# A transformer layer on one core: a feed-forward that begins with four token tiles, adds its partial products in PSUM and takes the gate a round earlier

## The chip, the core and the metric

The kernel runs on one core of a Trainium2 chip. The metric is device time in microseconds (us) of one execution; of several runs the median is shown. The engines are TensorE (PE, matrix products; PEld is its weight load), VectorE (DVE), ScalarE (ACT), GpSimd (POOL) and SyncE (SP), which issues the DMAs. Each engine works through its own list of instructions in a fixed order and waits on semaphores where it needs another engine's result. PE's results land in PSUM, eight banks of 512 fp32 values for each of 128 partitions; the other buffers are in SBUF, and parts of the program's data go to DRAM and back.

## What is computed

One layer of a diffusion backbone, batch 1, in fp32, for 512 sample tokens and 128 prompt tokens, with D_MODEL 1024 and D_FF 2816. Cut to its skeleton:

```python
mod = silu(cond) @ w_ada + b_ada                        # cond is c for the sample, c_ctx for the prompt
sh1, sc1, gt1, sh2, sc2, gt2 = split(mod, 6)
h = rmsnorm(x, norm_attn) * (1 + sc1) + sh1
q_lat, kv_lat, k_rope, gq, gk, gv, gf_low, gb_low, g_out = split(h @ w_in)
attn = attention(q_lat, kv_lat, k_rope)                 # 8 heads, low-rank keys and values
o = gla(gq, gk, gv, gates) * silu(g_out)                # gated linear attention, both directions
x = x + gt1 * (concat(attn, o) @ w_out)
h2 = rmsnorm(x, norm_ffn) * (1 + sc2) + sh2
a, g = split(h2 @ w_ffn_in, 2)                          # 2 x 2816 columns
x = x + gt2 * ((silu(a) * g) @ w_ffn_out)
y = rmsnorm(x, final_norm)
```

The outputs are y for prompt and sample, and the prompt's latent keys, rotary keys and final states. The change touches the loads of w_ada, the second norm, the feed-forward and the last gate.

## The kernel before

**Tokens and precision.** The 640 tokens are five tiles of 128: 0 to 3 are the sample, 4 is the prompt. Every fp32 factor is split in a rounded high part (a cast on ACT, L219) and a low part (a subtraction on DVE, L220), and a product is three passes: high by high, high by low, low by high (`mm3`, L212 to L214). A matrix product below always counts these passes.

**What sets the order.** The program is first written in a natural order. Then a planner (`Plan`) lays all instructions on the engines with a cost for each (`cost`) and a lag for each semaphore, redraws the order at random TRIES times in windows of 100 us and keeps the shortest; `keep` fixes that order on every engine. So a change in one place or in a cost can move instructions on all engines. SBUF is handed out by allocators: `late` names the ring of split weights that the feed-forward takes turns in (eight slots of 1024, TURNS), `rounded` the split activations, `plain` the rest.

**Up to 380 us.** Loads, adaLN modulation, first norm, input projection, gated linear attention, attention. Then the output projection: its first 512 columns for all tiles, its second 512 columns tile by tile in the order 4, 0, 1, 2, 3, 24 products each. After a tile's second half `residual` runs on DVE (L1365, L1366), then `second_norm(t)`: square with sum on ACT (L1417), the reciprocal root (two scalar steps on ACT, L278, five on DVE, L246 to L250), the scale on ACT (L1419), eight transposes on PE (L1429), scale and shift from PSUM on DVE and ACT (L1437, L1435), and the splits of four right operands (`right_split`; a right operand `right[r]` is a 512 x 320 piece of the normed activations: half of the features, half of the columns of each tile, 64 columns a tile). Differences of the pieces (L1447 to L1450) later give `right` 4 to 7.

**The feed-forward** takes the 2816 hidden columns in 22 pairs j of 128 columns (an a half for the silu and a g half), in rounds of 6, 6, 5 and 5 pairs (PARTS). Of the first CLASSIC pairs (2) each is computed by `whole`: four uses of a weight tile, a0, a1, g0, g1, for each 24 products of 128x320 (two PSUM halves times four k times three passes, L1560), 96 for a pair. All other pairs go through `part`: seven sub-products of 12 each (L1600), r = 1, 2, 6, 7, 5, 4, 3, by the scheme that multiplies 2x2 blocks with seven products, 84 for a pair. Each sub-product has a PSUM bank of its own; DVE adds it to sums in SBUF (L1604, seven per pair), ACT copies the first (L1607), ACT applies silu (L278), DVE multiplies a by g (L1627), and the product is split into hidden columns (`hidden_split`). `weights` splits the weight tiles up to eight uses ahead.

After each round its hidden columns are multiplied with w_ffn_out, 512 output columns at a time (n = 0, 1), with one PSUM bank per tile as accumulator (`mm3`, 128x512). The sums y over rounds are kept in DRAM: the second and third round load, add and store them. In the last round all y are loaded and multiplied by the gate gt2 and added to x (L1645, L1646, five tiles by two halves); n = 0 runs over pairs with all five tiles inside, n = 1 runs tile by tile, each followed by `final`: square (L1740), reciprocal root, one DVE step that scales by it and by final_norm (L1742), and the store. The last tile's n = 1 comes in two parts of 256 columns, with separate squares (L1753). The gate gt2 is made by `ada_gate(5)` in the second round and its vectors are loaded in the last.

## Time and profile before

| | |
|---|---|
| time, median of 3 runs | 831.02 us (830.35 to 831.64) |
| profiled execution | 831.04 us, its span 829.3 us |
| mean granted clock of PE | 0.983 |
| PE busy | 792.4 us, 96% of the span |
| PE weight loads | 703.1 us, 85% |
| DVE busy | 625.1 us, 75% |
| ACT busy | 387.1 us, 47% |
| moved by DMA | 118.17 MB, 142 GB/s in the mean |

The span is the time from the first to the last instruction in the profile; 1.7 us of the execution's time lie around it. A busy PE is not always PE at its peak: its products overlap, so the distance between starts counts, and the clock that the throttle grants it can be half. The chain of waits tells which work set the end at each time; windows tell how busy each engine was in a stretch and which clock PE had. A row of a timeline gives start, length, engine, line, operation, output and input, and in brackets the idle time before it with what ended it.

### The profile page before, as it was taken

The numbers are of one execution on the slowest core, as the hardware profiler recorded it, in microseconds if no ns is written. First come the engines' busy times: TensorE is split into PE (matmuls) and PEld (weight loads), VectorE is DVE, ScalarE is ACT, GpSimd is POOL, SyncE is SP. The second block draws the span as 40 slices with busy tenths as digits, with TensorE's granted clock in tenths as the row PEclk, the third lists the DMA queues.
The fourth block names the chain that finished last, engine by engine and source line by source line (L and its number), as shares of the span: only waits on it lengthen the run. The fifth ranks groups of instructions, "written<-read, shape, count | busy, mean of one in ns | idle before, by whom it ended". The sixth has DMA issues, their size and how long they took to land.

```text
span 829.3 us, 13015 instructions
## 1 busy us (share of the span) xinstructions
PE 792.4 (96%) x4803; PEld 703.1 (85%) x4803; DVE 625.1 (75%) x1252; ACT 387.1 (47%) x770; POOL 5.2 (1%) x15
## 2 busy tenths in 40 slices
PE   8899799899998999997999999999999999999994
PEld 6588787687987877886999988999879998899984
DVE  4689995886657565479888834888988886588897
ACT  6368255144556676258544434445214452245413
POOL 0000000000000000000000000000000000000000
PEclk9999999999999999997999999999999999999998
DMA  9981447327334246544132424333877335432433
GB/s 338 330 258 50 118 130 208 114 70 216 88 82 106 63 127 201 173 159 128 52 102 64 140 89 140 90 115 114 257 214 227 104 112 187 171 103 90 136 106 127
DMA packets 102136, 118.17 MB, mean 142 GB/s; under 512 B 15543, under 2 KB 69937, under 8 KB 102073
## 3 DMA queue, kind: packets, MB, share of 16 engines
q1 hardware_dynamic: 102073, 117.35, 45.6%
q8 instruction: 38, 0.62, 0.3%
q14 instruction: 25, 0.20, 0.1%
HBM read 96.96 MB, written 13.55 MB: 133 GB/s over the span
## 4 chain that ended last, share of the span: by engine, by line
PE 77%; DVE 12%; DMA 6%; ACT 3%; issue 2%; SPq 0%; ACTq 0%; DVEq 0%
PE psum L1600 30%; PE psum L212 10%; PE psum L214 10%; PE psum L213 10%; PE psum L1560 4%; PE psum L889 3%; PE psum L1241 2%; PE psum L1310 2%; DMA plain<-in_w_ada 1%; DVE plain L1646 1%; PE psum L712 1%; DMA plain<-in_w_in 1%; ACT plain L278 1%; DVE plain L1645 1%; PE psum L1296 1%
## 5 line engine op out<-in xcount | busy, mean ns | idle before, releaser
L1600 PE MATMUL psum<-rounded,late 128*128 128x320 f32 x1680 | 247.5, 309 | 0.0
L1600 PEld LDWEIGHTS psum<-rounded,late 128*128 128x128 f32 x1680 | 246.8, 188 | 0.3
L219 ACT CAST late<-plain 128x512 fp32r<-128x512 f32 (+2 forms) x204 | 123.7, 617 | 206.6 <-PE psum L214 78.4
L220 DVE TENSOR_TENSOR late<-plain,late 128x512 fp32r<-128x512 f32 (+3 forms) x204 | 137.8, 683 | 50.9 <-ACT late L219 48.5
L214 PE MATMUL psum<-late,rounded 128*128 128x512 f32 (+1 forms) x225 | 86.6, 385 | 0.0
L213 PE MATMUL psum<-late,rounded 128*128 128x512 f32 (+1 forms) x225 | 86.5, 384 | 0.0
L212 PE MATMUL psum<-late,rounded 128*128 128x512 f32 (+1 forms) x225 | 86.5, 384 | 0.0
L1604 DVE TENSOR_TENSOR plain<-plain,psum 128x320 f32<-128x320 f32 x140 | 66.1, 484 | 23.3 <-PE psum L1600 21.8
L213 PE MATMUL psum<-rounded 128*128 128x512 f32 (+2 forms) x212 | 77.8, 376 | 4.4 <-DVE rounded L220 4.4
L214 PE MATMUL psum<-rounded 128*128 128x512 f32 (+2 forms) x212 | 76.0, 377 | 0.0
L212 PE MATMUL psum<-rounded 128*128 128x512 f32 (+2 forms) x212 | 75.1, 380 | 0.7 <-DVE rounded L552 0.5
L219 ACT CAST rounded<-plain 128x256 fp32r<-128x256 f32 (+5 forms) x91 | 50.7, 582 | 46.1 <-DMA plain<-in_w_in 14.3
L220 DVE TENSOR_TENSOR rounded<-plain,rounded 128x256 fp32r<-128x256 f32 (+5 forms) x91 | 56.7, 642 | 20.5 <-ACT rounded L219 18.5
L278 ACT ACTIVATE plain<-plain 128x1 f32<-128x1 f32 (+7 forms) x111 | 37.9, 349 | 27.4 <-DVE plain L1604 20.7
L214 PEld LDWEIGHTS psum<-late,rounded 128*128 128x128 f32 x225 | 42.3, 188 | 9.2 <-issue 0.8
L212 PEld LDWEIGHTS psum<-late,rounded 128*128 128x128 f32 x225 | 42.3, 188 | 8.3
L213 PEld LDWEIGHTS psum<-late,rounded 128*128 128x128 f32 x225 | 42.3, 188 | 8.3
L213 PEld LDWEIGHTS psum<-rounded 128*128 128x128 f32 x212 | 40.5, 193 | 10.2 <-DVE rounded L220 4.6
L212 PEld LDWEIGHTS psum<-rounded 128*128 128x128 f32 x212 | 40.0, 193 | 8.9 <-DVE rounded L552 1.4
L214 PEld LDWEIGHTS psum<-rounded 128*128 128x128 f32 x212 | 40.6, 194 | 7.7 <-issue 2.5
L1241 PE MATMUL psum<-rounded 96*128 96x320 f32 x192 | 37.3, 322 | 2.5 <-ACT plain L278 1.3
L500 DVE SCALAR_TENSOR_TENSOR plain<-plain 128x1024 f32<-128x1024 f32 x28 | 34.6, 1279 | 0.8 <-DMA plain<-in_w_ada 0.8
(278 smaller groups left out, 1084.9 us busy)
## 6 DMA issues: line engine op xcount, KB each, us to landing
plain<-in_w_ffn_in SPq DMA_DIRECT2D x44, 512.0 KB, 4.7
plain<-in_w_ada SPq DMA_DIRECT2D x26, 512.0 KB, 4.4
plain<-in_w_ffn_out SPq DMA_DIRECT2D x44, 256.0 KB, 3.1
plain<-in_w_ada SPq DMA_DIRECT2D x8, 1024.0 KB, 6.0
y<-plain SPq DMA_DIRECT2D x30, 256.0 KB, 2.9
plain<-y SPq DMA_DIRECT2D x30, 256.0 KB, 3.5
early<-in_w_in SPq DMA_DIRECT2D x7, 512.0 KB, 6.7
early<-in_w_ada SPq DMA_DIRECT2D x6, 512.0 KB, 8.0
```

What stands on the lines that cost most here:

```text
L212: mm(out, lh, rh, start=start, stop=False)
L213: mm(out, lh, rl, start=False, stop=False)
L214: mm(out, ll, rh, start=False, stop=stop)
L219: self.nc.scalar.copy(hi, src).ins,
L220: self.nc.vector.tensor_tensor(lo, src, hi.bitcast(F32), op=ALU.subtract).ins,
L278: i = self.nc.scalar.activation(out, src, func, **more).ins
L500: nc.vector.scalar_tensor_tensor(m.ap, raw.ap, x, m.ap, op0=ALU.mult, op1=ALU.add)
L889: self.nc.tensor.matmul(out, w[:, a], act[:, b], start=start and i == 0, stop=stop and i == 2)
L1241: nc.tensor.matmul(pv[:, n], q[:, a * TS + P * t : a * TS + P * t + P], k[:, b * KEYS + 320 * n : b * KEYS + 320 * n + 320], start=i == 0, ...
L1560: nc.tensor.matmul(pv[:, h], wv[:, k, a], right[:, k, b], start=first and k == 0 and i == 0, stop=not first and k == 3 and i == 2,)
L1600: nc.tensor.matmul(ps, wv[:, k, a], right[:, k, b], start=k == 0 and i == 0, stop=k == 3 and i == 2)
L1604: add = lambda out, x: nc.vector.tensor_tensor(out, x, by_tile(ps), op=ALU.add)
```

## The change

- **Loads of w_ada** by `ada_rest` (two pieces of 1024 columns): 16 of 512 KB in a ring of twice as many half-size buffers, instead of 8 of 1 MB.
- **Column order.** The right operands and hidden columns keep the tiles in the order 4, 0, 1, 2, 3 (ORDER) instead of 0 to 4, so tile 3, which is normed last, has the last 64 of 320 columns.
- **Head.** For the uses a0 and a1 of pair 0 (HEAD), `whole` computes the first 256 columns (four tiles) in 24 products and the last 64 in 24 more.
- **CLASSIC** is 1 instead of 2: pair 1 goes through `part`.
- **Sums in PSUM.** `part` uses three banks per pair: X for r = 1, 6, 5, 3, Z for 7 and 4, Y for 2. A later sub-product adds into the bank of the earlier ones. ACT copies the bank after r = 1, 6 and 7 (`keep`, L1626 of the new kernel); DVE adds a copy after r = 2, 5 and 4 (L1622); after r = 3 the silu reads the bank itself.
- **Gate.** In the third round the sums y are multiplied by gt2 and added to x, which is loaded from and stored to DRAM for it. gt2's vectors are loaded there. The last round has no y.
- **Last round.** All ten weight tiles are split ahead, and each tile runs through both halves of the output columns, then `final`. The last tile has parts of 512, 256 and 256.
- **Planner.** 10 ns more for a product in fp32r, 16 redraws instead of 20.

In the new kernel the line numbers are a little higher: the transposes are L1431, the products of `whole` L1568 and of `part` L1617, the residuals L1367, L1368 and L1669, L1670, the scalings of the second norm L1421, its squares L1419, the shift L1439 and L1437, the multiply of a by g L1649, and `final` has L1764 and L1766.

The places in the order of which the prediction speaks follow. PE between the output projection (L212 to L214) and the feed-forward, before (late_19xx names the weight slot):

```order
L212 MATMUL psum<-rounded 128x512
L1429 MATMUL psum<-plain 128x128
L213 MATMUL psum<-rounded 128x512
L214 MATMUL psum<-rounded 128x512
L1429 MATMUL psum<-plain 128x128 x19
L1560 MATMUL psum<-rounded,late_1913 128x320
L1560 MATMUL psum<-rounded,late_1914 128x320
```

The last 19 transposes, among them those of tiles 2 and 3, stood ahead of every product of the feed-forward. The same place now:

```order
L214 MATMUL psum<-rounded 128x512
L1431 MATMUL psum<-plain 128x128 x8
L1568 MATMUL psum<-rounded,late_1922 128x256 x6
L1431 MATMUL psum<-plain 128x128
L1568 MATMUL psum<-rounded,late_1922 128x256
L1431 MATMUL psum<-plain 128x128 x3
L1568 MATMUL psum<-rounded,late_1922 128x256 x11
L1431 MATMUL psum<-plain 128x128 x2
L1568 MATMUL psum<-rounded,late_1922 128x256 x2
L1431 MATMUL psum<-plain 128x128 x2
L1568 MATMUL psum<-rounded,late_1922 128x256 x4
L1568 MATMUL psum<-rounded,late_1919 128x320
```

Tile 3's eight transposes now stand among the 24 four-tile products of a0; all 256-column products of a1 come behind them. DVE at the same place, from the scalar chain of tile 2's norm (L248 to L250) on, before:

```order
L248 TENSOR_TENSOR plain<-plain 128x1
L249 TENSOR_SCALAR plain<-plain 128x1
L250 TENSOR_TENSOR plain<-plain 128x1
L1437 TENSOR_SCALAR plain<-psum,plain 128x128
L1365 TENSOR_TENSOR plain<-psum,plain 128x512
L1366 TENSOR_TENSOR plain<-plain 128x512
```

and now:

```order
L246 TENSOR_SCALAR plain<-plain 128x1
L247 TENSOR_TENSOR plain<-plain 128x1
L1367 TENSOR_TENSOR plain<-psum,plain 128x512
L248 TENSOR_TENSOR plain<-plain 128x1
L249 TENSOR_SCALAR plain<-plain 128x1
L250 TENSOR_TENSOR plain<-plain 128x1
L1368 TENSOR_TENSOR plain<-plain 128x512
```

Tile 3's residual multiply moved ahead of the last three scalar steps of tile 2. DVE at the end, from the second last tile's scaling on, now (before, two scalings and the residuals of four tiles stood between each other in the last 20 us):

```order
L1766 SCALAR_TENSOR_TENSOR plain<-plain 128x1024
L1669 TENSOR_TENSOR plain<-psum,plain 128x512
L1670 TENSOR_TENSOR plain<-plain 128x512
L1669 TENSOR_TENSOR plain<-psum,plain 128x256
L1670 TENSOR_TENSOR plain<-plain 128x256
L1669 TENSOR_TENSOR plain<-psum,plain 128x256
```

Only the last tile's own residuals stand behind the scaling of the tile before it.

The diff, cut to its core:

```diff
--- before.py
+++ after.py
...
-        src = self.A["w_ada"].rearrange("(h k p) n -> k p h n", h=2, p=P)[:, :, :, D * q : D * q + D]
...
         for k in range(KD // 2):
-            raw = raws.take()
-            rv = raw.rearrange("p (h j c) -> p h j c", h=2, j=2)
-            nc.sync.dma_start(raw.rearrange("p (h n) -> p h n", h=2), src[k])
-            group = []
+            group, two = [], []
             for h in range(2):
+                raw = raws.take()
+                two.append(raw)
+                row = P * (k + KD // 2 * h)
+                nc.sync.dma_start(raw, self.A["w_ada"][row : row + P, D * q : D * q + D])
+                rv = raw.rearrange("p (j c) -> p j c", j=2)
...
-            raws.back(raw)
+            for raw in two:
+                raws.back(raw)
...
-        cols = 64 * t, 64 * t + 64
+        at = 64 * ORDER.index(t)
+        cols = at, at + 64
...
-            out = self.rb.alloc(1024, within=TURNS)
+            out = self.rb.alloc(1024, within=None if r in ROWS and j >= D_FF // P - PARTS[-1] else TURNS)
...
-        for h in range(2):
-            right = self.right[(1, 2, 0, 3)[2 * h + int(r[1])]].v("p (k s t) -> p k s t", k=4, s=2)
-            for k in range(4):
-                for i, (a, b) in enumerate(((0, 0), (0, 1), (1, 0))):
-                    nc.tensor.matmul(
-                        pv[:, h], wv[:, k, a], right[:, k, b],
-                        start=first and k == 0 and i == 0, stop=not first and k == 3 and i == 2,
-                    )
+        starts = []
+        for lo, hi in ((0, HALF - 64), (HALF - 64, HALF)) if (j, r) in HEAD else ((0, HALF),):
+            for h in range(2):
+                right = self.right[(1, 2, 0, 3)[2 * h + int(r[1])]].v("p (k s t) -> p k s t", k=4, s=2)
+                for k in range(4):
+                    for i, (a, b) in enumerate(((0, 0), (0, 1), (1, 0))):
+                        begin = first and k == 0 and i == 0
+                        ins = nc.tensor.matmul(
+                            pv[:, h, lo:hi], wv[:, k, a], right[:, k, b, lo:hi], start=begin and lo == 0,
+                            stop=not first and k == 3 and i == 2, skip_group_check=(0, r) in HEAD,
+                        ).ins
+                        if begin and lo == 0:
+                            starts.append(ins)
+                        elif begin:
+                            self.after(ins, starts[h])
...
-        pb = self.bank()
-        ps = pb.ap[:, :HALF]
+        place = "X" if r in (1, 6, 5, 3) else "Y" if r == 2 else "Z"
+        first, last = r in (1, 2, 7), r in (2, 3, 4)
+        if first:
+            s[place] = self.bank()
+        ps = s[place].ap[:, :HALF]
...
-                    ps, wv[:, k, a], right[:, k, b], start=k == 0 and i == 0, stop=k == 3 and i == 2
+                    ps, wv[:, k, a], right[:, k, b], start=first and k == 0 and i == 0,
+                    stop=k == 3 and i == 2, skip_group_check=not first,
...
+        def keep(x):
+            s[x] = sb.alloc(HALF)
+            nc.scalar.copy(s[x].ap, ps)
         if r == 1:
-            s["u2"] = sb.alloc(HALF)
-            nc.scalar.copy(s["u2"].ap, ps)
+            keep("p1")
             s["a"] = sb.alloc(T)
-        u2 = by_tile(s["u2"].ap)
-        if r == 2:
-            add(side("a", 0), u2)
+        elif r == 2:
+            add(side("a", 0), by_tile(s["p1"].ap))
             self.act(side("a", 0), side("a", 0), AF.Silu)
+            s.pop("p1").free()
         elif r == 6:
-            add(u2, u2)
+            keep("u2")
         elif r == 7:
+            keep("p7")
             s["g"] = sb.alloc(T)
-            add(side("g", 0), u2)
         elif r == 5:
-            add(u2, u2)
-            add(side("g", 1), side("g", 0))
+            add(side("g", 1), by_tile(s["p7"].ap))
+            s.pop("p7").free()
         elif r == 4:
-            add(side("g", 0), side("g", 0))
+            add(side("g", 0), by_tile(s["u2"].ap))
+            s.pop("u2").free()
         elif r == 3:
-            add(side("a", 1), u2)
-            self.act(side("a", 1), side("a", 1), AF.Silu)
+            self.act(side("a", 1), by_tile(ps), AF.Silu)
             f = s["a"].ap
             nc.vector.tensor_tensor(f, f, s["g"].ap, op=ALU.mult)
             self.hidden_split(j, f)
+        if last:
+            s.pop(place).free()
+        if r == 3:
             for x in self.pairs.pop(j).values():
                 x.free()
-        pb.free()
...
+            at = T * s + P * ORDER.index(t)
...
-            if last:
-                for m in self.right.values():
-                    m.free()
+            if p == len(PARTS) - 2:
                 for _ in gate:
                     pass
                 self.cond.free()
                 gt = [sb.alloc(D, True) for _ in range(2)]
                 for c in range(2):
                     nc.sync.dma_start(gt[c].ap, self.rows[1][c : c + 1].partition_broadcast(P))
+            if last:
+                for m in self.right.values():
+                    m.free()
                 fn = sb.alloc(D, True)
...
-                    for n in range(2):
-                        ns = slice(512 * n, 512 * n + 512)
-                        y = sb.alloc(512)
-                        nc.sync.dma_start(y.ap, yd[t][:, ns])
-                        residual(self.x[t].ap[:, ns], t, 512 * n, 512, y.ap)
-                        y.free()
+                self.weights(2 * count - len(self.ready))
+                ws = [self.use() for _ in range(2 * count)]
+                self.act_set(SET_EXP)
+                for t in range(NT):
+                    parts = [512, 512] if t < NT - 1 else [512, *LAST]
+                    done = 0
+                    for n_ in parts:
+                        pb = self.bank()
+                        cs, ys = slice(done % 512, done % 512 + n_), slice(done, done + n_)
+                        for i in range(count):
+                            wv = ws[done // 512 * count + i][1]
+                            self.mm3(
+                                pb.ap[:, :n_], hidden(first + i, 0, t), hidden(first + i, 1, t),
+                                wv[:, 0, cs], wv[:, 1, cs], i == 0, i == count - 1,
+                            )
+                        residual(self.x[t].ap[:, ys], t, done, n_, pb.ap[:, :n_])
+                        pb.free()
+                        done += n_
+                    self.final(t, fn, parts[1:])
+                return
...
                     for t in range(NT):
-                        if last:
-                            residual(self.x[t].ap[:, :512], t, 0, 512, acc[t].ap)
-                        else:
...
+                    y, dst = sb.alloc(512), yd[t][:, 512 * n : 512 * n + 512]
+                    if p == 0:
+                        nc.scalar.copy(y.ap, acc[t].ap)
+                    else:
+                        nc.sync.dma_start(y.ap, dst)
+                        nc.vector.tensor_tensor(y.ap, y.ap, acc[t].ap, op=ALU.add)
+                    if p < len(PARTS) - 2:
+                        nc.sync.dma_start(dst, y.ap)
+                    else:
+                        x, dst = sb.alloc(512), self.xd[t][:, 512 * n : 512 * n + 512]
+                        nc.sync.dma_start(x.ap, dst)
+                        residual(x.ap, t, 512 * n, 512, y.ap)
+                        nc.sync.dma_start(dst, x.ap)
+                        x.free()
+                    y.free()
+                    acc[t].free()
...
+        raws = Ring(sb, 2 * RING, D)
...
-CLASSIC, FIRST_USES, AHEAD_USES, RAW_AHEAD = 2, 3, 8, 8
+ORDER = 4, 0, 1, 2, 3
+HEAD = (0, "a0"), (0, "a1")
+CLASSIC, FIRST_USES, AHEAD_USES, RAW_AHEAD = 1, 3, 8, 8
...
+SWEEPS, TRIES, JITTER, WINDOW = 1, 16, 300, 1e5
...
         c = max(passes * n / 2.4, 53 * passes)
+        if passes == 1:
+            c += 10
...
```

More of the change, by code (lines that the diff above doesn't have):

```diff
@@ L442, in ada_rest @@
                     i = nc.tensor.matmul(
-                        pb.ap[r : r + 32], cv[:, h, k], rv[:, h, j],
+                        pb.ap[r : r + 32], cv[:, h, k], rv[:, j],
                         start=k == 0, stop=k == KD // 2 - 1, tile_position=(0, r),
@@ L1383, in output @@
         self.weights(FIRST_USES)
-        for t in (4, 0, 1, 2, 3):
+        for t in ORDER:
             pb = self.bank(1, ACC)
@@ new lines, in ffn @@
+                return
+            for n in range(2):
+                acc = [self.bank() for _ in range(NT)]
+                for j in range(first, first + count):
+                    self.weights(max(0, AHEAD_USES - len(self.ready)))
+                    w, wv = self.use()
+                    at += 1
+                    for t in range(NT):
+                        self.mm3(
+                            acc[t].ap, hidden(j, 0, t), hidden(j, 1, t), wv[:, 0], wv[:, 1],
+                            j == first, j == first + count - 1,
+                        )
+                    w.free()
+                    if p == GATE_PART:
+                        next(gate, None)
+                for t in range(NT):
+                    y, dst = sb.alloc(512), yd[t][:, 512 * n : 512 * n + 512]
[14 more added lines that the diff above has]
+                    acc[t].free()
@@ L1789, in early @@
         self.z_load(4)
-        raws = Ring(sb, RING, 2 * D)
+        raws = Ring(sb, 2 * RING, D)
         self.gvt = [sb.alloc(512, True) for _ in range(NT)]
@@ L1976 @@
 COLD = 3400
-SWEEPS, TRIES, JITTER, WINDOW = 1, 20, 300, 1e5
+SWEEPS, TRIES, JITTER, WINDOW = 1, 16, 300, 1e5
 def engine(ins):
```

45 lines of the change are left out of this document (1 added, 44 removed).

## The prediction

> **What bounds the kernel now.** I read the chain of waits first, for where the end is set, then PE's groups, then windows and timelines of the places that the change touches. The chain's rows from 389.10 us on (start, us, what):
>
> ```profile
> 389.10 29.63 PE psum L1560 x182
> 420.64 48.84 PE psum L1600 x333
> 722.73 61.61 PE psum L1600 x420
> ```
>
> The feed-forward is PE from its first product to the last rounds. 420 products of 320 columns in 61.61 us are 0.1467 us each. The windows (us, then PE, PEld, DVE, ACT, POOL busy, granted clock, DMA share, GB/s) show no slack in it:
>
> ```profile
> 400.00:500.00 100.00, 100.00 (x610) 94.71 (x609) 74.73 (x137) 43.81 (x83) 0.00 (x0) 1.00 0.30 93
> 500.00:600.00 100.00, 100.00 (x621) 95.49 (x620) 80.09 (x129) 44.63 (x79) 0.00 (x0) 1.00 0.47 144
> 600.00:700.00 100.00, 100.00 (x590) 92.02 (x589) 82.63 (x135) 37.20 (x66) 0.00 (x0) 1.00 0.57 177
> ```
>
> DVE and ACT have room everywhere, so taking adds from DVE is worth nothing by itself here. What is not PE at full speed lies at the two ends. First, the passage from the output projection to the feed-forward, on PE:
>
> ```profile
> 382.01 1.09 PE L1429 MATMUL psum<-plain 128*128 128x128 f32 x8 [1.24 <-ACT plain L1419]
> 385.71 1.97 PE L1429 MATMUL psum<-plain 128*128 128x128 f32 x8 [2.61 <-ACT plain L1419]
> 389.10 11.15 PE L1560 MATMUL psum<-rounded,late 128*128 128x320 f32 x56 [1.42 <-ACT rounded L219]
> ```
>
> PE waits 1.24 + 2.61 + 1.42 = 5.27 us for the norms of tiles 2 and 3, and the last row says that 56 products took 11.15 us where 56 x 0.1467 = 8.2 was due. The granted clock gives the reason, in windows of 3.41 us on the grid on which the clock changes in this trace:
>
> ```profile
> 142.59:146.01 3.42, 2.55 (x26) 0.99 (x18) 1.42 (x2) 3.08 (x4) 0.00 (x0) 1.00 0.76 196
> 146.01:149.42 3.41, 2.29 (x17) 1.74 (x18) 2.76 (x5) 0.77 (x2) 0.00 (x0) 0.98 0.93 309
> 149.42:152.83 3.41, 3.41 (x15) 3.02 (x13) 2.79 (x6) 0.41 (x1) 0.00 (x0) 0.52 0.74 290
> 381.50:384.92 3.42, 1.09 (x8) 0.85 (x8) 3.25 (x13) 3.13 (x8) 0.00 (x0) 0.98 0.69 202
> 384.92:388.33 3.41, 1.97 (x8) 1.57 (x8) 2.96 (x10) 2.88 (x7) 0.00 (x0) 0.50 0.34 109
> 388.33:391.74 3.41, 2.64 (x10) 2.64 (x11) 3.00 (x10) 3.01 (x10) 0.00 (x0) 0.50 0.84 239
> 391.74:395.15 3.41, 3.41 (x15) 3.41 (x14) 3.23 (x11) 0.71 (x2) 0.00 (x0) 0.52 0.29 71
> ```
>
> A window with PE busy 2.29 of 3.41 is followed by half clock, one with 2.55 is not; and of the windows at half clock 2.64 did not bring full clock back, 3.41 did. So PE ran at half speed from 389.10 to about 395.1: 3.0 us lost. The passage costs about 8 us. Second, the tail: PE's last product starts at 818.25 and ends at 818.53, but
>
> ```profile
> 818.25 0.28 PE L214 MATMUL psum<-late,rounded 128*128 128x256 f32 x1
> 796.00:803.00 7.00, 7.00 (x33) 5.79 (x31) 6.86 (x12) 0.00 (x0) 0.00 (x0) 1.00 0.00 0
> 803.00:810.00 7.00, 7.00 (x32) 5.82 (x31) 6.62 (x12) 2.38 (x7) 0.00 (x0) 1.00 0.01 2
> 820.01 1.28 DVE L1742 SCALAR_TENSOR_TENSOR plain<-plain 128x1024 f32<-128x1024 f32 x1
> 822.00 0.41 DVE L1645 TENSOR_TENSOR plain<-psum,plain 128x256 f32<-128x256 f32 x1
> ```
>
> DVE is full there (6.86 of 7) with the residuals of all tiles, and reaches the last piece of the last tile at 822.00, 3.47 us after PE was done. From there to the end of the span, 829.3, are 7.3 us that nothing in the change shortens.
>
> **The change, part by part.** The profiled execution took 831.04 us, the shown median is 831.02, so the sum is made against 831.04. I count PE's time as the moment from which it would have had to run at full speed without a stop.
>
> *Before:* 389.10 + 3.0 = 392.1.
>
> *Earlier start.* The new order puts tile 2's scalar chain on DVE (L248 to L250) behind tile 3's residual multiply (before: ahead of it) and tile 3's square on ACT behind tile 2's scale. These rows price it:
>
> ```profile
> 380.48 0.69 DVE L1365 TENSOR_TENSOR plain<-psum,plain 128x512 f32<-128x512 f32 x1 [0.24 <-PE psum L214]
> 380.81 1.15 ACT L1419 ACTIVATE plain<-plain 128x1024 f32<-128x1024 f32 x1
> ```
>
> Multiply to 381.2, three scalar steps of 0.2 to 381.8, scale 1.15: tile 2's transposes start at about 383.05 instead of 382.01. From a tile's transposes to the first product on it the old row shows 389.10 - 385.71 = 3.39, so the four-tile products of a0 start at about 386.4, 2.7 us sooner than the first product before. PE then has work until tile 3 is normed: 24 products of 256 columns and 8 transposes. Tile 3 itself comes 1 to 1.6 us later than before (about 390.0 to 390.7), and that work lasts longer, since the clock still drops: between 380.9 and 386.4 there are only 1.09 us of work, so whichever way the grid of 3.41 us falls, one window is under half busy. On the old grid the window to 388.33 is again partly idle, the one from 388.33 is full, and full clock is back at 391.74 instead of 395.15. Lost: (391.74 - 386.4) / 2 = 2.7. So 386.4 + 2.7 = 389.1, plus tile 3's eight transposes, now behind the start (1.09), 390.2.
>
> The Trainium skill ("TensorE: Matmul & The Clock Gate", the section on the clock gate and the one on HAM oscillation) has the array fall to half clock after an idle window of about 3.4 us. The trace agrees on the length of the window, not on idle: the longest gap here was 2.61 us and the clock fell. By the page's words it would not fall in the changed kernel; that is rival A.
>
> *Work in the feed-forward.* CLASSIC 1 makes pair 1 seven products of 12 instead of four of 24: 12 products fewer, -12 x 0.1467 = -1.8. The two head products are cut in 256 and 64 columns: 48 products become 96. The price of a product of 64 columns is not in the trace. Bounds, by these rows:
>
> ```profile
> 815.13 0.28 PE L212 MATMUL psum<-late,rounded 128*128 128x256 f32 x1
> 815.25 0.28 PE L213 MATMUL psum<-late,rounded 128*128 128x256 f32 x1
> L461 PE MATMUL psum<-plain x8: 172/253/253, 184.9 to 185.6; 128*128 128x4 f32 x8
> ```
>
> 256 columns start 0.12 apart, and by the step from 320 to 256 columns (0.0267) 64 would take 0.04; eight products of 4 columns, each with its own 128x128 weights, start (185.6 - 184.9) / 7 = 0.10 apart, where the weight load must set it. I take the middle, 0.07: 48 x (0.12 + 0.07 - 0.147) = +2.1, between +0.6 and +3.5. The Trainium skill ("TensorE: Matmul & The Clock Gate", the section on LDWEIGHTS) gives a load of 128 columns 128 / 1.2 = 107 ns; if that set the spacing, the same sum, an estimate by the page, would be +3.8, and the trace's 0.10 for a fresh load of 128 columns is close to it. The start then stands at 390.2 - 1.8 + 2.1 = 390.5: a gain of **1.6** (0.2 to 3.1 by the price of 64 columns).
>
> *Sums in PSUM.*
>
> ```profile
> L1604 DVE TENSOR_TENSOR plain<-plain,psum 128x320 f32<-128x320 f32 x140 | 66.1, 484 | 23.3 <-PE psum L1600 21.8
> ```
>
> Seven such adds per pair become three, and one copy on ACT becomes three. The adds go off an engine that PE did not wait for: 0. But product 6 now adds into the bank of product 1, 5 and 3 into it again, 4 into that of 7. PE must wait until ACT's copy (or DVE's add for 3) has read the bank; one other product lies between, 12 x 0.1467 = 1.76 us. The copy:
>
> ```profile
> 773.80 0.43 ACT L1607 COPY plain<-psum 128x320 f32<-128x320 f32 x1 [0.25 <-PE psum L1600]
> 771.16 1.14 ACT L219 CAST late<-plain 128x512 fp32r<-128x512 f32 x2 [2.17 <-PE psum L1600]
> ```
>
> About 0.25 to hear of PE, 0.43, and as much as 0.25 back: 0.9 when ACT is free, 1.45 with one cast (0.57) before it, 2.0 with two. Behind a late copy stand PE's whole stream, and nothing hides that. ACT is 40% busy and the new order keeps each copy next to its product, so I take +0.3 for the few late ones, from 0 to the price in rival C.
>
> *Gate in the third round.* Ten each of a load, multiply, add and store of 512 columns: 10 x 1.38 = 13.8 us DVE, which had 17.4 us free in 600 to 700 alone; 20 more DMAs of 256 KB where the DMA share is 0.57. Cost 0; if the adds held a bank that the second half's accumulators wait for, one such pair, +1.4. *Last round.* Tile by tile from its start, it needs the last pair's hidden columns after 12 products of 512 columns instead of 60. The rows of that chain:
>
> ```profile
> L278 ACT ACTIVATE plain<-plain 128x320 f32<-128x320 f32 x40 | 18.9, 471 | 20.9 <-DVE plain L1604 20.7
> L1627 DVE TENSOR_TENSOR plain<-plain 128x640 f32<-128x640 f32 x20 | 16.5, 824 | 0.0
> L219 ACT CAST rounded<-plain 128x640 fp32r<-128x640 f32 x22 | 16.0, 727 | 5.7 <-DVE plain L1627 5.7
> 813.65 0.39 PE L213 MATMUL psum<-late,rounded 128*128 128x512 f32 x1
> 814.56 0.39 PE L214 MATMUL psum<-late,rounded 128*128 128x512 f32 x1
> ```
>
> Four steps of 512 columns are 0.91 us, 0.2275 each, so 12 are 2.73. Silu 0.47, multiply 0.82 and cast 0.73 make 2.0, with three hand-overs of 0.25 2.8, and the subtract is needed one product later: +0.2 (0 to 0.8).
>
> *Tail.*
>
> ```profile
> L1646 DVE TENSOR_TENSOR plain<-plain 128x512 f32<-128x512 f32 x19 | 12.9, 691 | 0.6 <-DMA plain<-x 0.2
> 815.46 1.16 ACT plain L1740 x2
> 817.40 0.16 DVE L248 TENSOR_TENSOR plain<-plain 128x1 f32<-128x1 f32 x1
> ```
>
> Each tile now asks DVE for four residual steps of 0.69, the scalar chain (five steps of 0.2, from L246 to L250) and L1742's step (1.28): 5.0 us in the 6.8 of its 30 products, so no backlog. The order still puts the second last tile's L1742 ahead of the last one's residuals. The second last tile's products end 15 x 0.2275 + 30 x 0.12 = 7.0 before PE's end; its residual 1.4, square 1.2, the scalars on ACT and DVE 1.6 and the step 1.28 end 1.5 before it; then 1.4 for the last tile's first half and 0.8 for its third quarter: the last residual starts 0.7 after PE's end, not 3.47. Gain **2.8** (0 if that step comes 3 us later, 3.4 without any backlog).
>
> *Before the output projection*, smaller loads of w_ada and a newly drawn order of every engine. The chain there goes over DVE scans and DMAs:
>
> ```profile
> 84.74 1.49 DVE early L1040
> 94.90 5.39 DMA plain<-in_w_in
> 102.73 4.61 DMA plain<-in_w_in
> ```
>
> The order doesn't shorten a scan or a transfer, so 0; a window more or fewer at half clock is 1.7 us, and two of them are my bound either way, 3.4.
>
> **Sum:** -1.6 + 0.3 + 0.2 - 2.8 = -3.9, so 831.04 - 3.9 = **827.1 us**.
>
> **Rivals.** *A: the clock holds.* The 2.7 us lost at the start are not: 824.4. Against it: 2.29 of 3.41 was too little at 146. 5%. *B: the head gains nothing* (64 columns cost 0.10 and tile 3's norm comes 1 to 2 us later still, so that PE waits again before a1); only the tail pays: 831.04 - 2.8 + 0.5 = 828.7, to 830.5 when DVE's backlog stays in part. For it: DVE and ACT were both about 90% busy (3.25 and 3.13 of 3.42) in that passage, so all added work delays a norm. 16%. *C, the slower side: the banks.* Two casts ahead of a copy make 2.0 against 1.76: 0.25 us, and a copy that is late makes the freed weight tile, hence the next cast, late too. At 0.35 us per pair, 21 pairs, 827.1 + 7.4 = 834.5; it decides against the change from 0.19 us per pair on. For it: casts come in twos on ACT (row 771.16). Against: 60% idle ACT. 12%. *D: the redrawn early order* moves the time by one to two windows: 824 (9%) or 830.5 (9%). The forecast, 825.2 to 828.8, has 49%.
>
> **Numbers.** A measurement of this kernel tells 0.2%, 1.7 us, from no change: faster is below 829.4, slower above 832.7. Faster: 49 + 5 + 9 + 11 of B = 74%. Same: 5 of B + 7 of D = 12%. Slower: C and 2 of D, 14%. The range, 822.8 to 831.5, leaves out C and the ends of D.
>
> **What would show it.** Right: a first product of 256 columns near 386.4; full clock at about 391.7; products of 64 columns 0.05 to 0.09 apart; PE 100% busy from 400 to its end, with no wait of L1617 for L1626 or L1622; the last 256-column residual within 1 us of PE's last product. Wrong: PE idle between the four-tile products and a1 (B); waits of L1617 that come once per pair (C); a feed-forward that starts more than 2 us from 386 because the stages before it moved (D).

## The result: 0.55% slower, and the profile after

| | before | changed |
|---|---|---|
| time, median of 5 runs each | 831.41 us (830.35 to 832.53) | 835.73 us (835.27 to 836.68) |
| ratio to before | | 1.0055, 95% interval 1.004 to 1.0069 |
| span of the profiled execution | 829.3 us | 834.8 us |
| end of the output projection's last product | 380.44 us | 389.53 us |
| from there to PE's last product of all | 438.1 us | 437.6 us |
| from there to the end of the span | 10.8 us | 7.7 us |

The forecast was 827.1 us. The table cuts both traces at two points. Behind the output projection, where all edits of the feed-forward lie, the changed kernel is 3.6 us shorter (448.9 against 445.3). Ahead of it, where the forecast had put a zero with 3.4 us either way, it is 9.1 us longer. Both are read from one execution of each kernel. The last product of the output projection before:

```profile
380.05 0.39 PE L214 MATMUL psum<-rounded 128*128 128x512 f32 x1
```

The timeline of PE in the changed kernel at the passage (start, length, engine, line, operation, count, and in brackets the idle time before):

```profile
389.14 0.39 PE L214 MATMUL psum<-rounded 128*128 128x512 f32 x1
391.95 1.41 PE L1431 MATMUL psum<-plain 128*128 128x128 f32 x8 [2.42 <-ACT plain L1421]
394.88 1.89 PE L1568 MATMUL psum<-rounded,late 128*128 128x256 f32 x6 [1.52 <-ACT rounded L219]
```

Two gaps of 3.9 us together instead of three of 5.27. The windows (us; PE, PEld, DVE, ACT, POOL busy; granted clock; DMA share, GB/s) on the grid of this run's clock, for two places ahead of the output projection, for the passage, and of 100 us each in the feed-forward:

```profile
112.68:116.09 3.41, 1.47 (x3) 0.28 (x4) 3.41 (x11) 3.35 (x17) 0.39 (x1) 1.00 0.50 149
116.09:119.51 3.42, 2.87 (x10) 1.38 (x9) 3.34 (x25) 0.98 (x2) 0.56 (x1) 0.50 0.50 120
119.51:122.92 3.41, 3.41 (x16) 3.32 (x16) 2.73 (x9) 0.22 (x1) 0.00 (x0) 0.50 0.00 0
150.23:153.64 3.41, 0.19 (x4) 0.00 (x0) 0.83 (x1) 1.55 (x2) 0.00 (x0) 1.00 1.03 242
153.64:157.05 3.41, 2.81 (x11) 1.81 (x12) 2.13 (x4) 0.59 (x1) 0.00 (x0) 0.50 1.02 406
157.05:160.47 3.42, 3.42 (x16) 3.14 (x15) 1.40 (x4) 0.00 (x0) 0.00 (x0) 0.50 0.11 43
389.16:392.57 3.41, 0.99 (x8) 0.62 (x7) 3.26 (x12) 3.31 (x8) 0.00 (x0) 1.00 0.13 53
392.57:395.99 3.42, 1.90 (x9) 1.32 (x8) 3.18 (x14) 3.15 (x9) 0.00 (x0) 0.50 0.76 254
395.99:399.40 3.41, 3.41 (x18) 3.41 (x18) 1.89 (x6) 2.15 (x7) 0.00 (x0) 0.50 0.56 156
...
500.00:600.00 100.00, 100.00 (x621) 95.50 (x620) 68.91 (x104) 48.67 (x91) 0.00 (x0) 1.00 0.43 134
600.00:700.00 100.00, 100.00 (x590) 91.94 (x589) 78.09 (x113) 40.73 (x76) 0.00 (x0) 1.00 0.56 173
```

The passage has two windows at half clock instead of three, and the feed-forward is full. But in the early stages two idle stretches (1.47 and 0.19 busy of 3.41) are each followed by two windows at half clock. Over the whole stretch up to the output projection's end six windows are at half clock, before it was three. The groups of waits of PE there, the three longest (total in us, count, longest):

```profile
PE psum L1074 <- DMA plain<-plain: 3.2, 1, 3.2
PE psum L512 <- ACT plain L278: 3.0, 1, 3.0
PE psum L305 <- DMA early<-in_vecs: 2.8, 1, 2.8
```

Before, the longest was another one, and it was longer; so a list of waits alone doesn't show where the 9 us went:

```profile
PE psum L213 <- DVE rounded L220: 4.4, 1, 4.4
```

The steps of the chain behind the first wait of the changed kernel:

```profile
143.05 4.19 DMA plain<-plain
148.90 4.93 DMA plain<-plain
```

These transfers are the moves of the linear attention's gates (L1003, 64x640 values each). Before, the chain had one of them:

```profile
143.03 2.40 DMA plain<-plain
```

The moves go out in pairs, and these rows are not all of the same pair. By the rise of their semaphores the last pair took 2.4 and 2.5 us before and 5.1 and 4.9 now; the pair ahead of it 4.0 and 4.3 before and 3.8 and 4.2 now. So it is the last pair that became slower.

The tail of the changed kernel, the last rows of PE and DVE:

```profile
826.81 0.28 PE L214 MATMUL psum<-rounded 128*128 128x256 f32 x1
824.11 1.28 DVE L1766 SCALAR_TENSOR_TENSOR plain<-plain 128x1024 f32<-128x1024 f32 x1
827.43 0.42 DVE L1669 TENSOR_TENSOR plain<-psum,plain 128x256 f32<-128x256 f32 x1
```

The last residual starts 0.34 us after PE's end at 827.09, not 3.47.

### The profile page after: what moved, and what is told of

Its sections match the earlier page's. It is cut to its first block, busy times and chain, and to the rows that moved or that the text cites. A ratio compares the mean times of both kernels' runs of the same rounds, so it can differ in the third digit from the quotient of the medians.

```text
span 834.8 us, 13004 instructions
## 1 busy us (share of the span) xinstructions
PE 800.6 (96%) x4839; PEld 707.8 (85%) x4839; DVE 603.7 (72%) x1181; ACT 403.3 (48%) x816; POOL 4.8 (1%) x15
## 4 chain that ended last, share of the span: by engine, by line
PE 79%; DVE 9%; DMA 6%; ACT 3%; issue 2%; SPq 0%; ACTq 0%; DVEq 0%
PE psum L1617 31%; PE psum L212 10%; PE psum L213 10%; PE psum L214 10%; PE psum L891 3%; PE psum L1568 2%; PE psum L1243 2%; PE psum L1312 2%; PE psum L714 2%; DMA plain<-in_w_ada 1%; PE psum L1298 1%; DMA plain<-plain 1%; DMA early<-in_x_prompt 1%; DVE plain L502 1%; DVE rounded L220 1%
## 5 line engine op out<-in xcount | busy, mean ns | idle before, releaser
L1617 PE MATMUL psum<-rounded,late 128*128 128x320 f32 x1764 | 259.5, 309 | 0.0
L1617 PEld LDWEIGHTS psum<-rounded,late 128*128 128x128 f32 x1764 | 259.0, 188 | 0.2
L219 ACT CAST late<-plain 128x512 fp32r<-128x512 f32 (+3 forms) x205 | 125.8, 618 | 154.5 <-PE psum L214 86.3
L212 PE MATMUL psum<-rounded 128*128 128x512 f32 (+2 forms) x224 | 80.1, 377 | 2.6 <-DVE rounded L554 1.9
L212 PE MATMUL psum<-late,rounded 128*128 128x512 f32 (+1 forms) x213 | 82.4, 387 | 0.0
L214 PE MATMUL psum<-late,rounded 128*128 128x512 f32 (+1 forms) x213 | 82.3, 386 | 0.0
L213 PE MATMUL psum<-late,rounded 128*128 128x512 f32 (+1 forms) x213 | 82.3, 386 | 0.0
L213 PE MATMUL psum<-rounded 128*128 128x512 f32 (+2 forms) x224 | 81.5, 374 | 0.8 <-DVE rounded L220 0.8
L214 PE MATMUL psum<-rounded 128*128 128x512 f32 (+2 forms) x224 | 79.4, 372 | 0.0
L212 PEld LDWEIGHTS psum<-rounded 128*128 128x128 f32 x224 | 41.9, 191 | 10.9 <-DVE rounded L554 2.0
L1626 ACT COPY plain<-psum 128x320 f32<-128x320 f32 x63 | 27.0, 428 | 48.0 <-PE psum L1617 47.7
L214 PEld LDWEIGHTS psum<-rounded 128*128 128x128 f32 x224 | 42.1, 191 | 6.6 <-issue 0.8
L212 PEld LDWEIGHTS psum<-late,rounded 128*128 128x128 f32 x213 | 40.0, 188 | 8.8 <-issue 0.8
L213 PEld LDWEIGHTS psum<-rounded 128*128 128x128 f32 x224 | 42.1, 192 | 6.3 <-DVE rounded L220 1.1
L214 PEld LDWEIGHTS psum<-late,rounded 128*128 128x128 f32 x213 | 40.0, 188 | 8.3 <-DVE rounded L220 0.2
L213 PEld LDWEIGHTS psum<-late,rounded 128*128 128x128 f32 x213 | 40.0, 188 | 7.9
L1622 DVE TENSOR_TENSOR plain<-plain,psum 128x320 f32<-128x320 f32 x63 | 30.6, 486 | 13.2 <-PE psum L1617 9.8
```

Source lines behind the costliest of these rows:

```text
L212: mm(out, lh, rh, start=start, stop=False)
L213: mm(out, lh, rl, start=False, stop=False)
L214: mm(out, ll, rh, start=False, stop=stop)
L219: self.nc.scalar.copy(hi, src).ins,
L1617: nc.tensor.matmul(ps, wv[:, k, a], right[:, k, b], start=first and k == 0 and i == 0, stop=k == 3 and i == 2, skip_group_check=not first,)
L1622: add = lambda out, x: nc.vector.tensor_tensor(out, x, by_tile(ps), op=ALU.add)
```

## The experiments

Each table row below has the median, its ratio to the kernel before with the 95% interval where there is one, the end of the output projection and the rest of the span behind it. The last two are read from one profiled execution each. The kernel before has 831.0 to 831.8 in these comparisons, and for the profile 380.44 and 448.9.

**Whose order costs it.** The planner's order of all instructions written ahead of the output projection is taken from the other kernel (a table of their start times; everything else keeps its own order):

```diff
+            when[k] = times[g[-1]] if g[-1] < len(times) else t * here / there if t < there else t - there + here
...
+        row = self.sort({i: (when[i], rank[i]) for i in when}, before, after)
...
-        for k in sorted(range(gate), key=lambda k: (start[k], rank[k])):
+        for k in sorted(range(gate), key=lambda k: spot[k]):
```

> The changed kernel with everything that it computes, but with the instructions that are written ahead of the output projection in the order that the kernel before gives them on every engine; all later instructions keep the changed kernel's order. Theory 'order' (the redrawn order of the stages before the output projection cost some 9 us, the rest of the change gains 3 to 4): the output projection's last product comes back from 389.5 to about 380.5 us, no more than four windows of half clock before it, and the time is 831.4 - 3.6 = 827.8 us, between 826.5 and 829.5. Theory 'loads' (the 16 smaller loads of w_ada delay the early stages): they are still in, so the last product stays near 389 and the time at 835 to 836. Theory 'the local edits cost it': 835 to 836 too.

> The mirror of the first run: the kernel before, with its 1 MB loads, its feed-forward and its later order, but with the changed kernel's order of the instructions ahead of the output projection. Theory 'order': the last product of the output projection moves from 380.4 to about 389 us, three windows of half clock are added, and the time is 831.4 + 9 = 840 us, between 837 and 842. Theory 'loads' and theory 'the local edits cost it': 831.4 as before, give or take 1.

| | median | ratio | output projection ends | rest |
|---|---|---|---|---|
| changed, early order of before | 830.49 | 0.9978 (0.9965 to 0.9992) | 380.1 | 445.9 |
| before, early order of the changed | 845.22 | 1.0171 (1.0139 to 1.0202) | 394.5 | 448.1 |

The loss goes with the order and not with the edits: with the old early order the changed kernel is 5.2 us faster by the medians than as changed, and a little faster than before. The median is 2.7 us above the 827.8 that I expected, outside my range; the profiled execution, in which the output projection ends 9.4 us sooner, was 827.67, the fastest of ten. In the mirror the loss is 13.4, more than the 9 expected. The small loads cost nothing by themselves: under the old order, with them in, the output projection ends at 380.1, and the new order is worse with transfers of 1 MB than with halves (394.5 against 389.5).

**Was it the planner's new numbers, or the loads, or the draw?** Each of these draws all orders anew. The edits:

```diff
 e3, on the changed kernel
-        if passes == 1:
-            c += 10
-SWEEPS, TRIES, JITTER, WINDOW = 1, 16, 300, 1e5
+SWEEPS, TRIES, JITTER, WINDOW = 1, 20, 300, 1e5
 e4, on the changed kernel
-        raws = Ring(sb, 2 * RING, D)
+        raws = Ring(sb, RING, 2 * D)
...
 e5, on the kernel before
+        if passes == 1:
+            c += 10
 e6, on the changed kernel
-        if passes == 1:
+        if passes == 1 and any("late" in x.bass_ap.tensor.name for x in ins.ins if hasattr(x, "bass_ap")):
 g3 on the kernel before, g4 on the changed one
-        draw = random.Random(0)
+        draw = random.Random(1)
```

> The changed kernel with the planner's two numbers put back (no 10 ns more for a product, 20 redraws), so that all orders are drawn anew with the old costs. If the 10 ns lead the planner to a bad early order: the last product of the output projection near 381 and the time 827 to 829. If any redraw can land anywhere (theory 'order', with no part for the 10 ns): the last product anywhere from 379 to 391, and the time is that point plus 446 to 448 us (from the last product of the output projection to the end of the execution, as in the changed kernel). Theory 'loads': 835 to 836.

> The changed kernel with the loads of w_ada in 8 transfers of 1 MB again; planner, feed-forward and last rounds as changed; the order is drawn anew since the list of instructions differs. Theory 'loads': the last product of the output projection back near 381 and the time 827 to 828. Theory 'order': the 8 transfers change nothing by themselves, the last product lies where the new draw puts it, 379 to 391, and the time is that point plus 446 to 448.

> The kernel before with one edit: the planner counts 10 ns more for a product in fp32r; all orders are drawn anew. Theory 'the 10 ns lead the planner to worse early orders': the output projection's last product comes at 386 us or later instead of 380.4, with at least two windows of half clock more before it, and the time is 836 or more. Theory 'any redraw lands anywhere, the 10 ns have no part in it': no shift to the late side is owed; the last product between 376 and 386, the time between 827 and 837.

> The changed kernel, but the 10 ns are counted only for products that read a weight slot of the feed-forward's ring; the early products have the old cost. Theory 'the 10 ns': the early order is as good as the old one, the output projection's last product at 379 to 382 us and, with the changed kernel's 445 us from there to the end of the span, a time near 828, up to 833 with windows of half clock that differ from run to run. Theory 'any redraw lands anywhere': the last product anywhere from 377 to 392.

> The kernel before with another seed for the planner's 20 redraws, nothing else. If the order of the kernel before is one of many that are equally good: last product of the output projection at 379 to 382 us, time 830 to 833. If it is a lucky draw: last product at 384 or later, time 835 or more.

> The changed kernel with another seed for its 16 redraws, nothing else. If its planner numbers lead to late early stages in every draw: last product of the output projection at 386 us or later, time 832 or more. If its order was an unlucky draw: the last product anywhere from 379 to 392, and the time is that point plus 445 to 449 us.

| | median | ratio | output projection ends | rest |
|---|---|---|---|---|
| e3 changed, old numbers | 832.77 | 1.0007 (0.9993 to 1.0021) | 379.2 | 449.0 |
| e4 changed, old loads | 841.12 | 1.0113 (1.0089 to 1.0136) | 392.6 | 446.4 |
| e5 before, 10 ns | 833.64 | 1.0025 (1.0006 to 1.0045) | 385.0 | 447.5 |
| e6 changed, 10 ns only late | 838.03 | 1.0073 (1.0048 to 1.0097) | 385.3 | 450.6 |
| g3 before, other draw | 836.62 | 1.0058 (1.0032 to 1.0085) | 387.4 | 447.9 |
| g4 changed, other draw | 833.42 | 1.0028 (1.0011 to 1.0045) | 385.7 | 445.6 |

g3 decides that a draw alone is enough: the kernel before with nothing changed but the planner's seed ends its output projection 7 us later and is 0.58% slower, as much as the changed kernel. Of the eight draws (379.2, 380.4, 385.0, 385.3, 385.7, 387.4, 389.5, 392.6) the kernel before has the second earliest end and the changed kernel the second latest, so the first was a lucky draw and the other an unlucky one; the changed kernel's second draw (g4) is 2.3 us better. The draws with the 10 ns (389.5, 392.6, 385.0, 385.7) lie later than those without (380.4, 379.2, 387.4), 388.2 against 382.3 in the mean. e6, in which the early products have the old cost, ends at 385.3, where the theory that blames the 10 ns expected 379 to 382. With these few draws a share of the 10 ns is neither shown nor excluded. e3 shows that a draw can also lose at the passage: its early stages are the best of all, and PE then waits there for tile 2's scale (e6 has a wait of 5.4 us there too):

```profile
385.46 1.97 PE L1431 MATMUL psum<-plain 128*128 128x128 f32 x8 [5.37 <-ACT plain L1421]
```

**One place of the bad order.** In the changed kernel's order the fifth pair of w_ada loads (L439) and two loads of w_in go out ahead of the gates' last moves; before, the load that the pair replaces goes out behind them. Here all orders are read from a table of times, and the edit is in its numbers for this stretch: SP's transfers, and the products that use the pair, go to where the other order has them (in g2 the state updates on DVE that wait for loads move too).

```diff
+        times = np.cumsum(np.frombuffer(zlib.decompress(base64.b85decode(PINNED)), np.int32))
+        when = {k: times[g[-1]] for k, g in enumerate(groups)}
...
-        for k in sorted(range(gate), key=lambda k: (start[k], rank[k])):
+        for k in sorted(range(gate), key=lambda k: spot[k]):
```

> The changed kernel with its own order on every engine, except for one stretch: the fifth pair of w_ada loads of the second kind (L439) and the four products on it go back behind the moves of the linear attention's gates (L1003), and two loads of w_in go back ahead of them, as in the kernel before. In the changed kernel's trace the last two moves take 4.2 and 4.9 us to land instead of 2.4, PE waits 3.25 us for them at 153.7 and then runs two windows of 3.41 us at half clock. If that place is the main cause: the output projection's last product comes back from 389.5 to 383 to 385 us and the time from 835.7 to 829 to 831. If the loss is spread over many places of the early order: at most 2 us are won, 834 or more.

> The mirror: the kernel of the first run (changed kernel, early order of the kernel before) with that one stretch as in the changed kernel, the loads ahead of the moves and the four products of the fifth pair ahead of the gates' products; the state updates that wait for loads behind them come later too. If that place is the main cause: 4 to 7 us slower than the first run (830.5), 834.5 to 837, with a wait of 3 us for the moves and one or two windows more at half clock. If the loss is spread: within 2 us of it.

The good order with this stretch made bad (g2): 836.58 (1.0062, 1.0041 to 1.0082), 6.1 us slower than with the good one; the output projection ends at 389.0. Its PE there, and the chain's step:

```profile
148.08 3.10 PE L445 MATMUL psum<-plain 128*32 128x512 f32 x8 [3.62 <-DMA plain<-in_w_ada]
154.47 1.58 PE L1076 MATMUL psum<-plain 64*128 64x128 f32 x8 [2.29 <-DVE plain L1008]
```

```profile
145.54 7.96 DMA plain<-plain
```

So this place alone can cost 6 us: waits of 3.62 for the pair's own loads and of 2.29 behind the moves, a move that lands after 7.96, and three windows more at half clock (six against three). The loads stand closer to the moves here than in the changed kernel, whose slowest move took 5.1. The bad order with the stretch made good (g1) did not win it back: 840.07 (1.0102, 1.0072 to 1.0131), 4.3 us more than the changed kernel, with the end of the output projection at 393.6. There the two loads of w_in still went out between the two pairs of moves, since the first pair was ready only at 145.8, and the last one landed late as before:

```profile
145.80 2.47 DMA plain<-plain
149.93 5.01 DMA plain<-plain
```

The first move, ahead of which all bulk loads had landed, took 2.47; the one with two of them just ahead took 5.01. That the place was the main part of the changed kernel's own loss is therefore not shown; that such a place can cost that much is.

**What the head is worth.** On the first run's kernel, once with later orders drawn anew (e7, e8) and once with all orders kept (f1, f2):

```diff
-HEAD = (0, "a0"), (0, "a1")
+HEAD = ()                  e7, f2
+HEAD = ((0, "a0"),)        e8, f1
```

> The changed kernel with the early order of the kernel before (as in the first run), and HEAD empty: no product is cut in 256 and 64 columns, the feed-forward starts with all five tiles. From the trace of the changed kernel a product of 64 columns takes 0.110 us, so the 48 extra products cost 48 x (0.12 + 0.11 - 0.147) = 4.0 us, against some 3.2 us that the early start saves. If that account holds, this run is 0 to 2 us faster than the first run (830.5), 829.5. If the head pays as forecast (64 columns at 0.07), it is 1.5 to 3 us slower, 832 to 833.5.

> As the run before, but only a0 is cut (HEAD holds one use): 24 extra products of 64 columns instead of 48, and the same products in the gap before tile 3 is normed. By the account with 0.110 us: 2.0 us less PE work than with both uses cut, and the same start, so 2 us faster than the first run: 828.5, and the fastest of the four. If products of 64 columns cost 0.07: 1 us faster than the first run at most.

> The first run's kernel (changed kernel, early order of the kernel before) with all orders kept as they are there; the one edit is that a1 is not cut, its 24 products have 320 columns and follow a0's. 24 products of 64 columns fewer at 0.110 us: 24 x (0.12 + 0.11 - 0.147) = 2.0 us less for PE in a stretch where PE is the bound: 828.5 against the first run's 830.5, and the rest of the span after the output projection 444 us instead of 445.9. If 64 columns cost 0.07: 1.0 us. If the head's second cut was needed to cover tile 3's norm: PE waits before a1, and no gain.

> As the run before, with no cut at all: PE waits for tile 3's norm before its first product of 320 columns, all other orders are kept. From the trace of the first run: transposes of tile 3 near 387.2, first product near 390.5, half clock to about 395; that is a start as of 392.8 at full speed, against 385.46 + 2.9 + 1.0 + 48 x 0.083 = 393.4 with both cuts. So 0 to 1 us faster than the first run and 1 to 2 us slower than the run with a0 alone. If the head pays what was forecast (1.6 us and more), this run is at least 2 us slower than the first.

| | median | ratio | output projection ends | rest |
|---|---|---|---|---|
| both cut (e1) | 830.49 | 0.9978 (0.9965 to 0.9992) | 380.1 | 445.9 |
| e7 no cut, new draw | 831.66 | 0.9999 (0.9984 to 1.0014) | 383.7 | 445.5 |
| e8 a0 cut, new draw | 830.66 | 0.9992 (0.9974 to 1.0010) | 383.6 | 444.7 |
| f1 a0 cut, same order | 828.64 | 0.9970 (0.9956 to 0.9985) | 383.6 | 443.9 |
| f2 no cut, same order | 829.02 | 0.9978 (0.9964 to 0.9992) | 381.0 | 444.7 |

The rests of f1 and f2 are close to what was expected: 443.9 for 444, and no cut 1.2 us less than both cuts, for 0 to 1. So in these profiles cutting a0 gains 0.8 us of the rest, and cutting a1 as well loses 2.0. The medians of f1 and f2 differ by 0.4 us, less than they can resolve. The medians of e7 and e8 missed what was expected (829.5 and 828.5) by some 2 us; their output projections ended some 3 us later than e1's, more than the effect looked for. That need not come from the new draw: f1, with every order kept, ended as late. With the same early order the output projection ended at 380.1, 381.0 and 383.6 us, and that is the limit of all readings from one execution here. f1 is the fastest kernel of all, 0.30% under the kernel before and 0.8% under the changed one.

**What shortened the tail.**

```diff
 f3: the last round's first half pair by pair
+                for i in range(count):
+                    wv = ws[i][1]
+                    for t in range(NT):
+                        self.mm3(
...
-                    parts = [512, 512] if t < NT - 1 else [512, *LAST]
+                    parts = [512] if t < NT - 1 else LAST
 f4: the gate and the residuals of y back in the last round
+                        nc.sync.dma_start(y.ap, yd[t][:, ns])
+                        residual(self.x[t].ap[:, ns], t, 512 * n, 512, y.ap)
```

> The changed kernel with the early order of the kernel before, and the first half of the last round as before: pair by pair over five tiles, five residuals together, then the second half tile by tile; the gate stays in the third round. Reads the tail alone: from PE's last product to the end of the span before 10.8 us, changed 7.7. If running tile by tile makes the gain, the tail is 10 us or more; if taking the residuals of y out of the last round makes it, 7.7 to 8.5.

> The mirror of the run before: the last round tile by tile as changed, but the gate is loaded and the residuals of y are added in the last round as before. If taking the residuals of y out makes the gain, the tail from PE's last product is 10 us or more; if the tile by tile order makes it, 7.7 to 8.5; if both are needed, both runs have more than 8.5.

From PE's last product to the end of the span: f3 10.4 us, f4 8.4, both edits 7.7, before 10.8. Without tile by tile 2.7 of the 3.1 us are lost, without the earlier gate 0.7 (one execution each). f3's DVE is behind: when PE has ended (820.17) it has just begun the last tile's first piece, and the scaling of the tile before it comes 2.6 us later:

```profile
820.15 0.41 DVE L1671 TENSOR_TENSOR plain<-psum,plain 128x256 f32<-128x256 f32 x1
822.78 1.28 DVE L1779 SCALAR_TENSOR_TENSOR plain<-plain 128x1024 f32<-128x1024 f32 x1
```

## Why the prediction was wrong

**The step that failed** is "*Before the output projection* ... The order doesn't shorten a scan or a transfer, so 0; a window more or fewer at half clock is 1.7 us, and two of them are my bound either way". It measured +9.1. The three windows more at half clock are at most 3 x 3.41 / 2 = 5.1 us, and 4.5 when PE's busy time in them is halved (19.3 us in six against 10.2 in three); PE's idle time up to the output projection's end rose from 20.8 to 22.5 us, 1.7; some 2.9 us are in neither and stay open. The 9.1 itself is one execution against one, and one order was seen to move that point by 3.4; by the medians the old order wins back 5.2. Two assumptions of the step were false. A transfer does get longer by its place in the order: the last pair of the gates' moves went from 2.4 and 2.5 to 5.1 and 4.9 us. And the old chain, though it ran over scans and transfers, was no floor that a new draw keeps: the kernel before with another seed is 5.6 us slower. The prediction named this as rival D, with 9% on the slow side and 3.4 us as its price; the mechanism was there, its size in the profile was nearly three times that, and the range ended at 831.5 for it.

**The local sum** came out at -3.6 for -3.9 in this pair of profiles, which is in part luck. Its terms have errors that cancel (below). The four profiles with the old feed-forward (before, e2, e5, g3) have a rest of 447.5 to 448.9, and the pair took the longest; those with the changed one have 445.3 to 446.4 (as changed, e1, e4, g1, g2, g4), but 449.0 and 450.6 in two draws that lose at the passage (e3, e6). And with the early order held, the median gained 1.3 us (831.77 to 830.49; 0.7 to 2.9 by the interval), not 3.9. Where a typical execution loses the difference is open. Term by term:

- *Start.* Counted from the output projection's end, the first four-tile product came 0.6 us sooner than forecast (394.88 for 386.4 + 9.1), and the clock was back 1.4 us sooner than the old grid had it (399.4 for 391.74 + 9.1). Rival A fell: the clock did drop, after 0.99 busy of 3.41. The Trainium skill's rule ("TensorE: Matmul & The Clock Gate", HAM oscillation) of no idle gap over 3.4 us would have held the clock, since the longest gap was 2.42; the trace decides against it. But the argument against A, that 2.29 of 3.41 busy was too little, is no limit either: in the changed kernel's trace full clock stayed on after the window 256.04:259.45 with 1.84 busy.
- *64 columns*, the term that was mis-sized. The chain of the changed kernel:

```profile
401.35 15.10 PE psum L1568 x119
```

These are 48 products of 64 columns, 24 of 256 and 47 of 320. Less 24 x 0.12 and 47 x 0.147, 48 products take 5.3 us, 0.111 each. I had taken 0.07, and 0.10 as the upper end. So the cut cost 4.0 us for two uses instead of 2.1, and the rests of e1, f1 and f2 agree with it. The Trainium skill's LDWEIGHTS rule (same page, 128 / 1.2 = 107 ns for a load of 128 columns) gave +3.8, the better estimate, and the trace agrees with its 107 ns to 4 ns. That the weight load sets the distance is inferred from this; no run varied the load.
- *Head.* Rival B's condition, that PE waits again before a1, did not come: PE has no wait behind 395 us. Its outcome did: with both uses cut the rest is 1.2 us longer than with none (e1, f2). In the prediction's own terms the head was worth nothing already, 1.9 of earlier start for 2.1 of cuts; its gain of 1.6 comes from CLASSIC's 1.8, which the expectations of e7 and f2 count in where they speak of a head that pays.
- *Sums in PSUM*: +0.3 was taken, 0 measured. After 400 us the waits of PE list nothing at all, though ACT took 43 copies more. Rival C fell.
- *Last round and third round*: no wait, as costed (0.2 and 0).
- *Tail*: 3.1 for 2.8, since the second last tile's scaling ended 1.7 us ahead of PE's end instead of 1.5, and the residual steps behind it took 2.1 instead of 2.2; f3 and f4 show that it comes from the tile by tile order first.

## What to carry to other kernels

Where a planner draws the order, an edit anywhere is two edits: what it says, and a new draw of everything. Price the draw from several seeds of the old kernel before trusting any sum of a few us, and measure an edit with the rest of the order held. A product that brings its own 128-column weights cost 0.11 us here with 64 columns and 0.10 with 4, against 0.12 with 256, so cutting one to start it early has to save more than that.

## What the runs showed of the hardware

- A window of 3.41 us at half clock in which PE was busy 2.87 of 3.42 us, or 2.81 of 3.41, was followed by another at half clock, and a full one brought full clock back. The share alone doesn't decide: in e2 the window at 113.75 with 2.64 of 3.41 busy was followed by full clock, as was that of g2 at 147.56 with 2.89. Two windows at half clock cost up to 3.4 us on top of the wait ahead of them (3.25 us at 153.67 in the changed kernel).
- One and the same program varies: the twelve runs of f1 lie between 826.19 and 831.46 us, with a mean granted clock of 0.988 in the fastest and 0.982 in the slowest. One window at half clock is 0.002 of that mean, so the difference is about three windows.
- A move of 64x640 values took 2.4 to 2.6 us where the bulk loads issued ahead of it had landed or were about to, and up to 8.0 us where four of 512 KB had not. By the semaphores the moves landed behind the last of these loads: 0.8 us behind in the kernel before (load at 144.65, move at 145.43), 1.9 in the changed kernel (151.96, 153.83), 0.6 in g2 (152.88, 153.50).
